# P.V gathered over three pairs of key tiles, and ten neighbourhood P buffers

## The chip, the cores and the metric

The kernel runs on one core of one Trainium2 chip. The metric is the time of one execution in microseconds of device time. Three runs of the kernel before took 2532.98, 2533.22 and 2537.31 us; the median is 2533.22 us. The engines are named as in the profile: PE (matrix multiplication), PEld (its weight loads), DVE, ACT, POOL and SP.

## The reference

One layer over 2048 latent tokens (a grid of 32 rows by 64 columns) with 256 context tokens. Two token mixers run on the same modulated input and are merged, projected and added to the stream:

```
oa = block_attention(qa, concat(ka, kca), concat(va, vca), mla_scale)   # 8 heads, DK 96, DV 64, all 2048+256 keys
ob = neighborhood_attention(qb, kb, vb, c_kb, c_vb, rpb)                # 8 heads of 64, window 8x16 + 256 context keys
y  = (sigmoid(ga) * ((oa * silu(za)) @ w_oa) + sigmoid(gb) * ((ob * silu(zb)) @ w_ob)) @ w_out
out = rmsnorm(x + gate * y, final_g)
```

Both mixers are a softmax over scores followed by a product P.V with the values, all in float32 accuracy.

## The kernel before, in words

The program has three stages one after the other: the input projections (up to about 1055 us of the span), the two attentions (about 1055 to 2157 us), and the output projections. The change touches the attention stage alone.

**The large attention.** It is a loop over 32 units: 8 heads by 4 blocks of 512 queries. A unit goes through 18 tiles of 128 keys in 9 steps of a pair (`for kp in range(NKP)`). A step computes two score tiles `S` on PE (three matmuls each, the operands being split into a high and a low part), each read by ACT, which writes `exp` into the step's tile `P` (one of `PB = 8` buffers). POOL adds `P` to the running sum `za` (line 1288). In the same steps PE computes `pm`, the scores of the next unit, 20 tiles of 512 or 256 columns spread over steps 0 to 5, and DVE takes their maxima `m` (line 825). From these DVE folds, POOL spreads (`md`, line 812) and PE makes the row `pmf` in step 8, which the next unit's scores need.

**P.V.** `pv(u, kp, ...)` is called one step late, for the pair of the step before. It puts the pair into the list `late`, and when `kp % PVB == PVB - 1`, or at the last pair, it issues the matmuls of every listed pair into `acc`. A pair's two tiles go to partitions 0 to 63 and 64 to 127 of `acc`, each with a stationary operand 64 columns wide, so the two run beside each other in the two column halves of the array. Every other matmul of the steps has a stationary operand 128 columns wide, but for sums over `za` (`zp`, `nz`), which are 32 wide. A float32 matmul shows as two instructions in the trace, so a pair is four `oacc` instructions.

**The neighbourhood attention** is a generator, `natten`, whose work is fed into the same steps by weight (`feed`): per head 24 maxima tiles `nm` with 8 `nc`, four spreads `nmd` on POOL each followed by a matmul `nf`, then 24 score tiles `ns` in 12 pairs. A score tile becomes a tile `np` (tag `P` of the pool `npl`, `NPB` buffers of 2 KB a partition), which POOL adds to `nza`. Its P.V, `n_pv` (result `no`), is 64 wide too. A pair first waits in `queue` behind the next pair, then in `held`; after each burst of P.V the loop empties `held` behind it, and where more than `HELD = 2` pairs are held, the oldest is issued at once. At the end of a head what is left is issued, the result is copied out, and the next head's keys and queries are loaded.

**Order.** PE's instructions of the loop are kept in program order (`pe["pin"]`). The other engines' orders are a planner's. Score tiles of every kind rotate through five PSUM buffers (`psm`: three of `psM`, two of `psS`), so PE waits when the tile five places back has not yet been read. `acc` has one buffer.

With `PVB = 2` a unit's P.V is issued behind the scores of steps 2, 4, 6, 8 and of step 0 of the next unit, with 2, 2, 2, 2 and 1 pairs.

Of the kernel before, what the change touches and what calls it, by code (L numbers as in the profile page):

```python
# [48 lines left out]
LEAD = 3  # L49
TAIL = 6  # L50
FILL = 16
PVB = 2
X0P = True
NATP = (2, 4)
STAT0 = 300
# [1 line left out]
HELD = 2  # L57
PB = 8
ZDVE = {1: tuple(range(1, 9))}
NPB = 6  # L60
BIG = -float(2 ** 100)


# [1 line left out]
def tile_hybrid_layer(ctx: ExitStack, tc: tile.TileContext, I: dict, out: bass.AP, dbg=None):  # L65
# [74 lines left out]
    def psm(name):  # L140
        if env["rot"] is not None:
            env["rot"] = (env["rot"] + 1) % 5
            if env["rot"] >= 3:
                return env["psS"].tile([P, W], F32, tag="S", name=name)
        return psM.tile([P, W], F32, tag="M", name=name)
# [778 lines left out]
    def n_score(d, t):  # L924
        h = d["h"]
        ps = psm(f"ns{h}_{t}")
        pt = npl.tile([P, W], F32, tag="P", name=f"np{h}_{t}", bufs=NPB)
        za = d["za"]
# [300 lines left out]
    def pv(u, kp, pt, acc, za, vt):  # L1229
        late.append((kp, pt))  # L1230
        if kp % PVB == PVB - 1 or kp == NKP - 1:
            env["burst"] = True
# [311 lines left out]
```

## Time and profile before

| | us |
|---|---|
| median of three runs | 2533.22 |
| profiled execution | 2537.19 |
| its span, first to last instruction | 2535.4 |
| PE busy in the span | 2489.2 (98%) |
| POOL / DVE / ACT busy in the span | 1093.5 / 1105.9 / 903.1 |
| mean granted TensorE clock | 0.995 |

The profile is of one execution on the chip. Busy times of PE come from modelled ends: matmuls are pipelined, so a matmul of 512 columns shows 0.40 us, while the next one starts 0.23 to 0.24 us after it. What PE spends is therefore read from the starts. Idle time of an engine costs something only where another engine waits for it.

### The profile page before, as it was taken

What the parts mean: (1) busy time and instruction counts of PE and PEld (TensorE: products, weight loads), DVE (VectorE), ACT (ScalarE), POOL (GpSimd) and SP (SyncE); (2) the same over time, 40 slices, a digit from 0 to 9 for tenths busy, and PEclk for the clock granted to TensorE, in tenths of its full rate; (3) what the DMA queues carried; (4) which work ended last, traced back from release to release, by engine and by line L of the source; (5) the groups of instructions that cost most, each with busy time, mean ns of one, the idle gap of its engine ahead of it and who ended that gap; (6) DMA issues with size and microseconds to landing.
All of it is one profiled execution on the core that took longest, in us unless ns stands there. A gap on an engine that the chain in (4) does not pass through costs nothing.

```text
span 2535.4 us, 34849 instructions
## 1 busy us (share of the span) xinstructions
PE 2489.2 (98%) x12796; PEld 1833.4 (72%) x12796; DVE 1105.9 (44%) x2285; ACT 903.1 (36%) x1774; POOL 1093.5 (43%) x861
## 2 busy tenths in 40 slices
PE   7999999999999999999999999999999999999998
PEld 4878888877789888756566656565656564888998
DVE  4654221222311211255465545465545446455654
ACT  4664432212322122234444444444444444112221
POOL 1312111111310000268877878777878886133220
PEclk9999999999999999999999999999999999999999
DMA  7535766456652466631415141514150333755542
GB/s 269 191 94 166 253 225 193 126 164 192 191 167 89 121 208 209 177 85 47 100 33 129 39 110 39 121 38 110 39 129 15 76 135 123 262 184 164 179 146 71
DMA packets 182979, 342.86 MB, mean 135 GB/s; under 512 B 25130, under 2 KB 95950, under 8 KB 175438
## 3 DMA queue, kind: packets, MB, share of 16 engines
q1 hardware_dynamic: 168872, 299.01, 39.5%
q0 software_dynamic: 13504, 41.35, 5.8%
q8 instruction: 100, 1.64, 0.3%
q14 instruction: 71, 0.58, 0.1%
q10 hardware_dynamic: 432, 0.28, 0.0%
HBM read 214.42 MB, written 126.13 MB: 134 GB/s over the span
## 4 chain that ended last, share of the span: by engine, by line
PE 89%; DMA 3%; DVE 3%; SPq 1%; ACT 1%; issue 1%; POOL 1%; POOLq 0%; DVEq 0%; ACTq 0%
PE accm L135 26%; PE S L807 15%; PE oacc L807 10%; PE pm L807 6%; PE f L135 5%; PE ya L135 4%; PE vacc L135 4%; PE nacc L226 3%; PE no L807 3%; PE accf L135 2%; PE accx L135 1%; PE nm L807 1%; DMA rz<-rzS 1%; PE pstl L185 1%; PE qa_False L135 1%
## 5 line engine op out<-in xcount | busy, mean ns | idle before, releaser
L1288 POOL TENSOR_TENSOR za<-za,P 128x1024 f32<-128x1024 f32 x217 | 516.3, 2379 | 111.2 <-ACT P L1278 107.5
L825 DVE TENSOR_REDUCE m<-pm 128x1 f32<-128x512 f32 (+1 forms) x640 | 388.1, 632 | 327.2 <-PE pm L807 320.6
L1278 ACT ACTIVATE P<-S 128x512 f32<-128x512 f32 x576 | 342.1, 596 | 452.4 <-PE S L807 432.7
L135 PE MATMUL accm<-hh,whi 128*128 128x512 f32 x928 | 366.8, 395 | 0.0
L135 PE MATMUL accm<-hl,whi 128*128 128x512 f32 x928 | 366.5, 395 | 0.0
L135 PE MATMUL accm<-hh,wlo 128*128 128x512 f32 x928 | 366.5, 395 | 0.0
L807 PE MATMUL oacc<-P,V 128*64 128x512 f32 x1152 | 286.7, 614 | 0.0
L807 PE MATMUL S<-qh,Kh 97*128 97x512 f32 x576 | 238.5, 414 | 3.9 <-DVE m L825 1.5
L807 PE MATMUL S<-ql,Kh 96*128 96x512 f32 x576 | 229.5, 398 | 0.0
L807 PE MATMUL pm<-Kh,qh 96*128 96x512 f32 (+1 forms) x640 | 223.5, 388 | 4.9 <-ACT P L1278 2.7
L807 PE MATMUL S<-qh,Kl 96*128 96x512 f32 x576 | 228.3, 396 | 0.0
L135 PEld LDWEIGHTS accm<-hh,whi 128*128 128x128 f32 x928 | 174.2, 188 | 42.8 <-issue 0.8
L135 PEld LDWEIGHTS accm<-hh,wlo 128*128 128x128 f32 x928 | 174.2, 188 | 42.4
L135 PEld LDWEIGHTS accm<-hl,whi 128*128 128x128 f32 x928 | 174.2, 188 | 41.4
L135 PE MATMUL ya<-u,woh 128*128 128x256 f32 x1024 | 185.0, 283 | 1.7 <-DVE t L1346 1.7
L807 PEld LDWEIGHTS pm<-Kh,qh 96*128 96x128 f32 x640 | 120.2, 188 | 90.5 <-issue 37.5
L807 PEld LDWEIGHTS oacc<-P,V 128*64 128x64 f32 x1152 | 69.5, 137 | 134.4 <-issue 133.6
L135 PE MATMUL f<-wfh,y 128*128 128x512 f32 (+1 forms) x528 | 161.6, 386 | 5.0 <-ACT y L1349 2.9
L135 PEld LDWEIGHTS ya<-u,woh 128*128 128x128 f32 x1024 | 160.1, 192 | 2.9 <-DVE t L1346 2.1
L135 PE MATMUL ya<-u,wol 128*128 128x256 f32 x512 | 144.9, 283 | 0.0
L807 PEld LDWEIGHTS S<-qh,Kh 97*128 97x128 f32 x576 | 109.4, 190 | 48.3 <-issue 16.9
L356 ACT ACTIVATE g<-accm 128x512 f32<-128x512 f32 x88 | 52.1, 592 | 249.5 <-PE accm L135 201.9
(1928 smaller groups left out, 4248.9 us busy)
## 6 DMA issues: line engine op xcount, KB each, us to landing
rawc<-in_wch SPq DMA_DIRECT2D x30, 512.0 KB
KA<-kB SPq DMA_DIRECT2D x16, 576.0 KB
xl<-in_xb SPq DMA_DIRECT2D x32, 256.0 KB
wm<-in_wmodb SPq DMA_DIRECT2D x8, 1024.0 KB
kmS<-sk POOLq DMA_DIRECT2D x32, 256.0 KB, 3.7
qR<-q SPq DMA_DIRECT2D x16, 512.0 KB
qm<-sq POOLq DMA_DIRECT2D x32, 256.0 KB, 3.9
woS<-ps SPq DMA_DIRECT2D x16, 512.0 KB
```

The source lines that it names most:

```text
L135: nc.tensor.matmul(acc, a, b, start=(i == 0), stop=(i == n - 1))
L185: nc.tensor.matmul(pst[32 * j:32 * j + 32, :w], ones[:, 0:32], sq[:, :w], start=(kt < 4), stop=(kt >= 4))
L226: nc.tensor.matmul(acc[:, :n], a[:, k, sl], b[:, k, :n], start=(k == 0 and q == 0), stop=(k == KT - 1 and q == 2))
L356: nc.scalar.activation(s1, acc, AF.Sigmoid)
L807: ins = nc.tensor.matmul(*args, **kw)
L825: nc.vector.reduce_max(m5[:, qt, ci:ci + 1], pm[:, :b - a], axis=AX.X)
L1278: nc.scalar.activation(pt[:, x, :], sp, AF.Exp)
L1288: ve.tensor_tensor(za, za, pt, op=ALU.add)
```

## The change

Two constants change. P.V is issued after three pairs, with 3, 3 and 3 pairs a unit, behind the scores of steps 3 and 6 and of step 0 of the next unit. The neighbourhood's `P` has ten buffers, 8 KB a partition more.

```diff
-PVB = 2
+PVB = 3
...
-NPB = 6
+NPB = 10
```

## Rows read from the trace of the kernel before

**Rows 1.** The page: span, PE's busy line, the chain that ended last.
```profile
span 2535.4 us, 34849 instructions
PE 2489.2 (98%) x12796; PEld 1833.4 (72%) x12796; DVE 1105.9 (44%) x2285; ACT 903.1 (36%) x1774; POOL 1093.5 (43%) x861
...
PE 89%; DMA 3%; DVE 3%; SPq 1%; ACT 1%; issue 1%; POOL 1%; POOLq 0%; DVEq 0%; ACTq 0%
```

**Rows 2.** Engines by stretch, the part of the loop with neighbourhood work.
```profile
core 0: us, PE busy (x) PEld busy (x) DVE busy (x) ACT busy (x) POOL busy (x), PEclk, DMA share, GB/s
...
1090.00:2100.00 1010.00, 998.75 (x4927) 614.60 (x4925) 543.06 (x1099) 451.81 (x816) 807.22 (x482) 0.99 0.31 78
```

**Rows 3.** Waits of PE, 1055 to 2157 us: total, times, longest us.
```profile
PE nf L807 <- POOL nmd L812: 3.9, 3, 2.7
PE pmf L807 <- POOL md L812: 3.2, 1, 3.2
PE pm L807 <- ACT P L1278: 2.7, 4, 0.7
PE pm L807 <- DVE m L825: 1.8, 3, 0.8
```

**Rows 4.** Timeline of PE (start, us, instruction, count): two pairs between wide matmuls.
```profile
1525.18 0.39 PE L807 MATMUL S<-ql,Kh 96*128 96x512 f32 x1
1525.42 0.39 PE L807 MATMUL S<-qh,Kl 96*128 96x512 f32 x1
1525.64 0.39 PE L807 MATMUL pm<-Kh,qh 96*128 96x512 f32 x1
1525.96 1.94 PE L807 MATMUL oacc<-P,V 128*64 128x512 f32 x8
1527.83 0.50 PE L807 MATMUL pm<-Kh,qh 96*128 96x512 f32 x1
1528.17 0.30 PE L807 MATMUL ns_('w', 0, 0)_12607<-QQ,KA 128*128 128x288 f32 x1
```

**Rows 5.** Timeline: one pair alone; two pairs with a neighbourhood pair.
```profile
1517.74 1.94 PE L807 MATMUL oacc<-P,V 128*64 128x512 f32 x8
1519.51 0.59 PE L807 MATMUL no<-np_('c', 0, 1)_12355,nv 128*64 128x512 f32 x1
...
1520.46 0.39 PE L807 MATMUL pm<-Kh,qh 96*128 96x256 f32 x1
...
1614.15 1.08 PE L807 MATMUL oacc<-P,V 128*64 128x512 f32 x4
1615.16 0.50 PE L807 MATMUL pm<-Kh,qh 96*128 96x512 f32 x1
```

**Rows 6.** Engines in three stretches of one unit between two bursts.
```profile
1511.91:1517.74 5.83, 5.83 (x28) 4.56 (x26) 5.17 (x11) 3.12 (x6) 2.35 (x1) 1.00 0.11 25
1520.46:1525.96 5.50, 5.50 (x27) 4.35 (x26) 4.58 (x10) 2.51 (x5) 3.13 (x2) 1.00 0.00 0
1527.83:1533.20 5.37, 5.37 (x29) 4.08 (x29) 4.14 (x10) 2.75 (x6) 4.66 (x3) 1.00 0.01 3
```

**Rows 7.** Timeline of PE at the first nf; idle before it in brackets.
```profile
1103.67 0.79 PE L807 MATMUL nf<-nmd,onesr 128*128 128x512 f32 x1 [2.67 <-POOL nmd L812]
```

**Rows 8.** PE busy, granted clock and DMA by stretch, after that and at 1618.
```profile
1103.70:1106.70 3.00, 3.00 (x7) 0.50 0.86 172
1106.70:1109.70 3.00, 3.00 (x9) 0.54 0.00 0
...
1618.00:1624.00 6.00, 4.68 (x16) 0.79 0.57 155
```

**Rows 9.** Waits in the loop: the longest for neighbourhood P.V.
```profile
DVE np_('w', 1, 3)_16453 L953 <- PE no L807: 4.4, 1, 4.4
```

**Rows 10.** Engines by stretch, while a head's operands are loaded.
```profile
1839.00:1863.00 24.00, 24.00 (x134) 13.69 (x133) 8.88 (x17) 11.03 (x19) 19.62 (x12) 1.00 1.01 231
```

**Rows 11.** The page's group of DVE's maxima: busy, mean ns, idle before.
```profile
L825 DVE TENSOR_REDUCE m<-pm 128x1 f32<-128x512 f32 (+1 forms) x640 | 388.1, 632 | 327.2 <-PE pm L807 320.6
```

## The prediction

> **What bounds the kernel now.** I read the page first: the profiled execution has a span of 2535.4 us (its own time is 2537.19, so 1.8 lie around the span), PE is busy for 98% of it and holds 89% of the chain that ended last [rows 1]. The reader is to see there that time can only be won on PE. The engines by stretch come next, for the attention loop: POOL is busy 807.2 of 1010 us, DVE 543.1, ACT 451.8, at a granted clock of 0.99 [rows 2]. They have slack, POOL the least with 20%. The waits of PE say how much of the loop is not PE's own work: the four largest sums are 3.9, 3.2, 2.7 and 1.8 us in 1102 us [rows 3]. So the loop, 1102 of the 2535 us, is a queue of matmuls in a fixed order, and its length is the sum of the distances from one start to the next. The timeline of PE gives these, and it is where the change is decided.
>
> **Part 1, PVB: what a separate burst costs.** Wide matmuls of 512 columns follow each other at (1525.64 - 1525.18) / 2 = 0.23 us. The first P.V matmul starts 0.32 after the last wide one: 0.09 lost on the way in. The first wide one after the burst is followed by the next at 0.34 instead of 0.23: 0.11 lost behind it [rows 4]. The burst itself, from its first start to the next wide start: one pair takes 1615.16 - 1614.15 = 1.01, two take 1527.83 - 1525.96 = 1.87, two with a neighbourhood context pair (as much work as a third) take 1520.46 - 1517.74 = 2.72 [rows 4, 5]. That is 0.855 a pair and a remainder of 0.155 that does not grow with the length. A burst costs 0.09 + 0.155 + 0.11 = 0.355 us whatever it holds; I take 0.35. Four starts read to 0.01 us put it between 0.33 and 0.37. No other engine can hide it: PE has no idle time there, it is the array that changes between 64 and 128 wide.
>
> The Trainium skill says of this change of width that "Changing tiling mode (not just tile) drains the TensorE" (TensorEngine Tiling (Array Packing), Key Properties). TensorE: Matmul & The Clock Gate (Single matmul latency, Back-to-back issue gap) gives an isolated matmul (398 + N) / 2.4 ns and one in a stream N / 2.4 + 2.5, so that a drain would be some 163 ns and a burst with two of them 0.33 us, an estimate; the sum would be 61 x 0.33 = 19.9 us. The trace has 0.355, and I go by it.
>
> **How many bursts go.** Walked through the loops as written: before, 32 units x 5 = 160 bursts, the last two with nothing between them, so 159; 7 of the 8 flushes of neighbourhood P.V at a head's end stand alone: 166. After: 32 x 3 = 96; the 8 head ends then all stand alone, and once a third pair is held (HELD = 2) and goes out by itself: 105. So 61 go, and 61 x 0.35 = 21.4 us (20.1 to 22.6). The matmuls themselves are the same in number and kind, so nothing else changes in PE's own work. The bursts of 32-wide sums (zp, nz) stay.
>
> **The longer stretch between bursts.** During a burst DVE and ACT catch up; between bursts PE produces score tiles that they must read within five tiles. In three two-step stretches DVE worked 5.17 of 5.83, 4.58 of 5.50 and 4.14 of 5.37 us [rows 6]: always below PE, so a third step adds no backlog on average. What is new is steps 1 to 3 in one stretch. They hold 10 maxima against 7 in steps 1 and 2; the third step's 3 cost DVE 3 x 0.632 = 1.9 us [rows 11], and with a neighbourhood share (DVE's 543.1 us [rows 2] over 288 x 1010 / 1102 = 264 steps are 2.05 a step, less 2.2 maxima, 0.65) 2.55, about what PE needs for half a two-step stretch (2.7). The second group, steps 4 to 6, ends with a step without maxima. Bounds: a loss of as much again as PE waits for ACT and DVE in the rows, 2.7 + 1.8 = 4.5 [rows 3], or a gain of 4.5 where the present waits fall into longer bursts. I take a loss of 1.5, since DVE's share is nearer to full than to half.
>
> **The matmuls nf and pmf, which wait for POOL.** POOL spreads the maxima, and PE then waits at nf (3.9 us in all) or pmf (3.2) [rows 3]. For pmf the distance holds: the burst of step 6 lies between in both kernels, and it has three pairs instead of two. For nf, walked again, 7 of 32 have a burst between spread and matmul now, 4 after. Three lose their cover. Below, nothing; above, three waits as long as the longest, 2.67 [rows 7]. Behind that wait the granted clock was 0.50 and 0.54, that is 1.2 GHz for nearly all of 6 us [rows 8], which loses some 2.9. So 3 x 5.6 = 16.8 above. I take 1, because 3 waits in 32 are listed now though 25 have no cover. Queued behind a waiting nf is all of PE, and through it everyone.
>
> **Part 2, ten buffers.** With bursts further apart up to eight neighbourhood tiles are alive at once (counted in the same walk), so six would not do. The longest wait of DVE for such a buffer was 4.4 us [rows 9]; with ten these waits go. DVE is not PE's bound there, so the gain is between 0 and the 1.8 for which PE waits for DVE [rows 3]; I take 0, as none of those waits names such a tile. The 8 KB lie in a pool that is closed before the output projections, and no instruction or transfer is added.
>
> **The loads at a head's end.** They are issued behind the head's last scores, as before. In one head they kept the DMA engines at 1.01 for the 24 us up to the next head's first scores [rows 10]. The transfers do not get faster while PE comes earlier: 24 us are about 6.3 steps of 3.8 us, which hold 3.5 bursts now and 2.1 after, 1.4 x 0.35 = 0.5 us. Seven heads at most: 0 to 3.5 us; I take 0.5, one head as tight as this one. SP's and POOL's queues get nothing new, and no queue is passed. The end of the loop is unchanged: the last two bursts already are one.
>
> **The sum**, against the profiled execution: 2537.2 - 21.4 + 1.5 + 1 + 0 + 0.5 = 2518.8. That execution is 4.0 above the median of 2533.2, so the forecast is 2514.8, about 2515 us, or 0.7% faster.
>
> **Rivals.**
> 1. *The reads become the bound.* In steps 1 to 3 DVE falls behind, and PE stops at the fifth tile. For it: DVE at 89% in the first row [rows 6], and waits of about 0.6 us for it (1.8 in three) [rows 3]. Against: the other two stretches, 83 and 77%. Price: one such wait in half of the 64 stretches that hold maxima, 32 x 0.6 = 19 us; with the other terms 2534, no change.
> 2. *Idle PE loses its clock: slower.* Three idle places in the loop already did: [rows 8] show two of them. If the spreads on POOL (80% busy now, 82% at the shorter loop) come later than PE at nf and pmf, each event costs 2.67 + 2.9 = 5.6 us. The forecast's 18.4 are gone from the fourth new event (22.4), and with five the kernel is at 2515 + 28 = 2543. Place: the 63 nf and pmf matmuls. Against: pmf keeps its cover.
>    The Trainium skill has the same in TensorE: Matmul & The Clock Gate (HAM oscillation): an idle array falls back to half rate, and only activity releases it. The 0.50 of the rows agrees.
> 3. *The bursts do not merge.* If more than two pairs were held nearly always, neighbourhood P.V would go out by itself, and every such pair would cost the 0.35 that was won; 61 of the 96 pairs would do it, and the time would be 2533. Against: the walk finds one.
> 4. *Better than forecast.* Of the present waits most vanish, with a lucky order on DVE: another 8 us, 2507 or below.
>
> **How the numbers follow.** Forecast 0.80, rivals 1 to 4: 0.06, 0.05, 0.04, 0.05. The forecast's own range: downwards the burst's price (1.2) and the waits (1.5 + 4.5) to 2508; upwards the waits (3), one new clock event (5.6) and late loads (2) to 2526. That holds 8 in 10 by itself: 2508 to 2526. A measurement of this kernel tells about 0.2%, 5 us, from no change, so faster means below 2528: the forecast, rival 4 and a little of rival 1, 0.86. Within 0.2%: most of rivals 1 and 3 with a fifth of rival 2, 0.10. Slower: the rest of rival 2, 0.04.
>
> **What would show it.** P.V in runs of 12 instructions; no run of 4 or 8 inside the loop; the distances 0.32, 0.34 and 0.855 a pair unchanged, so that a run of three pairs lasts 2.72. The loop, from first score to last P.V, 18 to 21 us shorter than 1102, and the other two stages the same to 1 us. If the loop's shortening is smaller, PE's waits for DVE m or ACT P must have grown by it (rival 1), or POOL nmd and md with more time at clock 0.50 (rival 2). The forecast is wrong if the 0.35 does not go with the burst, that is if a run of three pairs takes longer than 2.72.

## The result and the profile after

The changed kernel takes 2520.27 us, median of its runs (2518.12 to 2524.23), against 2534.36 for the kernel before (2532.98 to 2537.31). The ratio is 0.9943, 95% interval 0.9929 to 0.9956: 14.1 us faster, 0.56%. The forecast was 2515, 18.4 faster. The direction, the size to within 5 us and the price and number of the bursts were right; two terms of the sum were not, and part of the nearness is luck, as the last parts show.

The profiled execution took 2524.23, 13.0 less than the one of before. First the page of the changed kernel: span, busy times, the chain's shares and the group of DVE's maxima.

```profile
span 2522.5 us, 34848 instructions
PE 2476.6 (98%) x12796; PEld 1841.1 (73%) x12796; DVE 1108.0 (44%) x2285; ACT 900.8 (36%) x1774; POOL 1092.7 (43%) x861
...
PE 91%; DVE 3%; DMA 2%; ACT 2%; issue 1%; POOL 1%; SPq 0%; POOLq 0%; ACTq 0%; DVEq 0%
...
L825 DVE TENSOR_REDUCE m<-pm 128x1 f32<-128x512 f32 (+1 forms) x640 | 385.9, 632 | 284.4 <-PE pm L807 278.0
```

Beside [rows 1, 11]: the same 12,796 matmuls and 12.6 us less of PE's busy time. DVE, ACT and POOL differ by at most 2.3 us, the weight loads show 7.7 more. A maximum still takes 632 ns.

Next the timeline of PE in the changed kernel around one burst (start, us, instruction, count), beside [rows 4]:

```profile
1120.70 0.40 PE L807 MATMUL S<-qh,Kl 96*128 96x512 f32 x1
1120.93 0.40 PE L807 MATMUL pm<-Kh,qh 96*128 96x512 f32 x1
1121.26 2.79 PE L807 MATMUL oacc<-P,V 128*64 128x512 f32 x12
1123.98 0.50 PE L807 MATMUL pm<-Kh,qh 96*128 96x512 f32 x1
1124.32 0.39 PE L807 MATMUL ns_('c', 2, 1)_9052<-QQ,KA 128*128 128x512 f32 x1
```

Three pairs are one run of 12. It begins 0.33 after the last wide matmul, lasts 1123.98 - 1121.26 = 2.72, and the second wide one behind it starts 0.34 after the first: the entry, the length and the exit that the prediction named. Counted over the loop there are 166 runs before and 105 after, as walked. The price of a run beyond its pairs, worked out from the starts of all runs that stand between wide matmuls, has a median of 0.349 us before and 0.350 after, for one, two and three pairs alike.

The waits of PE in the changed kernel, 1055 to 2157 us (total, times, longest), beside [rows 3]:

```profile
PE pm L807 <- DVE m L825: 5.8, 3, 3.5
PE S L807 <- ACT P L1278: 5.1, 6, 2.4
PE pm L807 <- ACT P L1278: 2.7, 4, 0.7
PE nf L807 <- POOL nmd L812: 2.1, 2, 1.9
PE S L807 <- DVE nmx L886: 1.1, 1, 1.1
```

POOL's waits shrank (nf 3.9 to 2.1, pmf 3.2 to none on the list). Those of `pm` for DVE's `m` grew from 1.8 to 5.8, and those of `S` for ACT's `P` from 0.4 to 5.1. Summed over all tiles, PE's waits went from 7.1 to 2.1 for POOL, from 4.8 to 8.4 for DVE and from 4.0 to 8.2 for ACT. The readers of PSUM have taken POOL's place.

**Where the 13 us lie.** By first score and last P.V, the profiled span splits into: before the loop 1055.6 to 1053.0 (-2.5), the loop 1100.8 to 1093.6 (-7.3), the output stage 379.0 to 375.9 (-3.1). The first is no effect of the change: before had a half-clock stretch of 3.4 us in its first stage, and among all executions of this study, whose first stages are the same code, it lasted 1050.9 to 1057.8. The loop holds -21.3 of bursts (61 x 0.35) and +14.0 of something else. Most of that are intervals between wide matmuls that are longer than the 0.23 of a stream. What they have too much, worked out from all starts, sums to 32.9 us before and 45.2 after:
- short ones at full clock, 60 to 200 ns too long: 81 (8.7 us) before, 122 (12.9 us) after, +4.2;
- long ones at full clock, over 200 ns: +4.6 in units 30 and 31 (5.7 to 10.3), +0.8 in all the others (16.3 to 17.1);
- intervals inside half-clock stretches: 1.9 to 4.0, +2.1; what is under 60 ns, +0.6.

The other 1.7 are bursts and narrower matmuls, in half-clock stretches mostly. Unit by unit the loop shows the same: units 0 to 27 are 15.6 us shorter, units 28 to 30 0.5, and unit 31, the last, is 8.9 us longer.

**The last two units.** The timeline of the changed kernel there, all engines, the lines that matter (idle before an instruction and what ended it in brackets):

```profile
2099.39 2.56 DVE L1106 TENSOR_TENSOR o<-o,z 128x256 f32<-128x256 f32 x1
...
2102.14 0.62 DVE L825 TENSOR_REDUCE m<-pm 128x1 f32<-128x512 f32 x1
...
2102.82 0.58 PE L807 MATMUL pm<-Kh,qh 96*128 96x256 f32 x1 [3.46 <-DVE m L825]
...
2123.28 0.42 DVE L1106 TENSOR_TENSOR o<-o,z 128x256 f32<-128x256 f32 x1 [0.32 <-DMA o<-oaS]
2123.74 0.42 ACT L1108 ACTIVATE u<-o 128x256 fp32r<-128x256 f32 x1 [1.34 <-DVE o L1106]
2124.18 2.07 ACT L1278 ACTIVATE P<-S 128x512 f32<-128x512 f32 x4
2124.82 0.50 PE L807 MATMUL S<-qh,Kh 97*128 97x512 f32 x1 [2.37 <-ACT P L1278]
...
2132.95 0.42 ACT L1108 ACTIVATE u<-o 128x256 fp32r<-128x256 f32 x1 [2.69 <-POOL o L1106]
2133.27 1.07 ACT L1278 ACTIVATE P<-S 128x512 f32<-128x512 f32 x2
2133.91 0.80 PE L807 MATMUL S<-qh,Kh 97*128 97x512 f32 x1 [1.83 <-ACT P L1278]
```

The reader is to see one pattern three times: a small instruction of the *next* stage stands in a reader's queue ahead of the work that PE waits for. `o`, `z` and `u` (lines 1105 to 1109, in `make_u`) prepare operands of the output projections, beside the last units. At 2102.82 (unit 30) PE had waited 3.46 for a maximum that stood behind DVE's `o`, and 1.60 at 2098.86 for another behind the `o` of 2095.90; before, the waits for DVE in that unit were 0.67, 0.63 and 0.43. In unit 31 there are no maxima any more, so the three-step stretch holds nothing but score tiles, each for ACT. ACT stood idle 1.34 and 2.69 us at a copy `u` whose `o` had not come, with the exps behind it, and PE ran out of its five buffers: 2.37 and 1.83 us. TensorE: Matmul & The Clock Gate, Part 1 (Architectural detail), in the Trainium skill, says that ACT's queue is strictly first in, first out; these rows agree, as the exps start 0.44 and 0.32 us after the copy, four and two in a row.

What followed on PE in the changed kernel, by stretch (PE's busy us first, then the other engines, granted clock, DMA):

```profile
core 0: us, PE busy (x) PEld busy (x) DVE busy (x) ACT busy (x) POOL busy (x), PEclk, DMA share, GB/s
2122.00:2125.00 3.00, 0.63 (x3) 0.19 (x3) 2.01 (x5) 1.64 (x4) 0.00 (x0) 1.00 0.50 158
2134.00:2140.50 6.50, 6.50 (x16) 2.97 (x18) 3.98 (x3) 2.67 (x6) 3.47 (x4) 0.50 0.36 111
```

In the first stretch PE is busy for 0.63 of 3 us. After the second idle place it worked for 6.5 us at a granted clock of 0.50, that is 1.2 GHz, with 16 matmul records in it. So 4.2 us of waits cost some 3.3 more (an estimate, half of the 6.5). In all, the loop spends 17.1 us at half clock before and 27.3 after. The wait of 3.2 for `pmf` in unit 30 of before [rows 3], with 6.8 us of half clock behind it, is gone; that is why unit 30 comes out even.

Part of it is given back behind the loop: the first final projection of before waits for a weight load, and after it does not. The row of before's output stage, then that of after:

```profile
PE f L135 <- DMA wfh<-wfS: 2.0, 1, 2.0
```

```profile
PE f L135 <- DMA wfl<-wfS: 0.5, 2, 0.3
```

What differs is when SP issues that load: at 2164.92 before, 8.5 us after the last P.V, and at 2151.00 after, 4.4 behind it. SP has the preparation of the next stage and the last store of `oaS` ahead of it in its queue, and in the changed kernel, whose last unit is 8.9 us longer, it is through with that earlier against the loop's end. Where the last unit is as short as before (e3, e4, e10), the issue is 9.0 to 10.6 us behind the last P.V and the wait is back.

### The profile page after: what moved, and what is told of

Its sections match the earlier page's. It is cut to its first block, busy times and chain, and to the rows that moved or that the text cites. A ratio compares the mean times of both kernels' runs of the same rounds, so it can differ in the third digit from the quotient of the medians.

```text
span 2522.5 us, 34848 instructions
## 1 busy us (share of the span) xinstructions
PE 2476.6 (98%) x12796; PEld 1841.1 (73%) x12796; DVE 1108.0 (44%) x2285; ACT 900.8 (36%) x1774; POOL 1092.7 (43%) x861
## 4 chain that ended last, share of the span: by engine, by line
PE 91%; DVE 3%; DMA 2%; ACT 2%; issue 1%; POOL 1%; SPq 0%; POOLq 0%; ACTq 0%; DVEq 0%
PE accm L135 26%; PE S L807 16%; PE oacc L807 10%; PE pm L807 5%; PE ya L135 5%; PE f L135 4%; PE vacc L135 4%; PE nacc L226 3%; PE no L807 3%; PE accf L135 2%; PE accx L135 1%; PE nm L807 1%; PE pstl L185 1%; PE qa_False L135 1%; ACT P L1278 1%
## 5 line engine op out<-in xcount | busy, mean ns | idle before, releaser
L807 PE MATMUL oacc<-P,V 128*64 128x512 f32 x1152 | 274.9, 613 | 0.0
L807 PE MATMUL pm<-Kh,qh 96*128 96x512 f32 (+1 forms) x640 | 214.5, 382 | 8.7 <-DVE m L825 5.8
L807 PEld LDWEIGHTS oacc<-P,V 128*64 128x64 f32 x1152 | 75.7, 139 | 150.1 <-issue 150.1
L807 PEld LDWEIGHTS S<-qh,Kh 97*128 97x128 f32 x576 | 109.5, 190 | 56.8 <-ACT P L1278 22.6
```

The lines of the kernel that those rows point to most:

```text
L807: ins = nc.tensor.matmul(*args, **kw)
```

## The experiments

"Loop" is first score to last P.V of the profiled execution (before 1100.8, changed 1093.6), "short" the number and sum of the short intervals at full clock (before 81 and 8.7, changed 122 and 12.9; the expectations counted those inside half-clock stretches too, 89 and 138). The time is a ratio to the kernel before on the same chip, with its interval.

| run | P.V bursts | ratio | loop, us | short (us) |
|---|---|---|---|---|
| e1_pvb1 | 294 | 1.0092 [1.0077, 1.0107] | 1129.6 | 21 (2.1) |
| e2_npb10 | 166 | 0.9985 [0.9976, 0.9994] | 1097.9 | 82 (8.7) |
| e3_last2 | 108 | 0.9924 [0.9911, 0.9936] | 1082.4 | 116 (12.5) |
| e4_ucopy | 105 | 0.9917 [0.9904, 0.9931] | 1081.8 | 122 (13.0) |
| e5_before_ucopy | 166 | 0.9990 [0.998, 1.0] | 1097.7 | 81 (8.7) |
| e6_pvb5 | 75 | 0.9921 [0.9908, 0.9934] | 1083.6 | 136 (14.5) |
| e7_merge678 | 136 | 0.9961 [0.9946, 0.9976] | 1091.3 | 88 (9.5) |
| e8_after | 105 | 0.9935 [0.9921, 0.9949] | 1094.9 | 120 (12.8) |
| e9_moredve | 105 | 1.0142 [1.0119, 1.0164] | 1133.8 | 277 (30.6) |
| e10_last2_ucopy | 108 | 0.9933 [0.992, 0.9946] | 1082.3 | 116 (12.4) |
| e11_pvb5_last2_ucopy | 80 | 0.9914 [0.9898, 0.9929] | 1082.0 | 135 (14.6) |

**e1: every pair alone** (on the kernel before).
```diff
-PVB = 2
+PVB = 1
```


> The kernel before with PVB = 1: every pair is its own burst. Walked through the loops, 294 separate bursts of 64-wide matmuls in place of 166, 128 more. Theory A (a burst costs 0.35 us whatever it holds): 128 x 0.35 = 45 us more than before, about 2579, with one pair still lasting 1.01 us from its first start to the next wide matmul. Rival B (the price is hidden or shared where bursts are short, or the gain of the change came from something else than the number of bursts): clearly less than 45, say under 25 us.

2561.89 against 2538.19, +23.7. The price held: its timeline shows a burst of one pair in the same form,

```profile
1506.65 0.40 PE L807 MATMUL S<-qh,Kl 96*128 96x512 f32 x1
1506.98 1.08 PE L807 MATMUL oacc<-P,V 128*64 128x512 f32 x4
1507.99 0.50 PE L807 MATMUL S<-qh,Kh 97*128 97x512 f32 x1
1508.33 0.40 PE L807 MATMUL S<-ql,Kh 96*128 96x512 f32 x1
```

0.33 in, 1.01 long, 0.34 out, and over 193 such bursts the median is 0.348: 128 x 0.348 = 44.6 us added. But what the longer intervals of wide matmuls have too much fell from 32.9 to 17.1, so 15.8 of it did not show, and the loop is 28.8 longer (1129.6 to 1100.8). The time is up by less, and meets the mark of rival B (under 25). The trace says in which sense: the price itself is not hidden in PE, but waits go as bursts come. That is what the prediction's sum also lacked: bursts give the readers time, and taking them away brings waits.

**e2: the ten buffers alone** (on the kernel before).
```diff
-NPB = 6
+NPB = 10
```


> The kernel before with ten neighbourhood buffers alone (PVB stays 2). Theory A: PE's order is the same and the waits for such buffers are not PE's, so no change, within 2 us of before. Rival C (the buffers carry part of the gain, or of the loss): more than 4 us either way.

0.9985, some 3.8 us (1.5 to 6.1). The waits of [rows 9] are gone: five of DVE and ACT for PE to free a buffer, 14.6 us in all. PE's order is the same instruction for instruction, its short waits stay (82), and the units differ from before by more than 0.1 us in six places: units 1 (-1.1), 12 (+1.6), 16 (-1.6), 27 (-1.0), 30 (-3.0) and 31 (+2.1). In units 1, 12, 16 and 30 a half-clock stretch falls elsewhere; in unit 31 two new waits of 0.71 and 0.84 stand before P.V. In unit 30 PE's clock fell at 2110.4, ahead of `pmf`, which then came in time, instead of after a wait for it; e5 has -2.6 there with six buffers.

Unit 27 is the place of the buffers. The timeline of the kernel before:

```profile
2006.67 0.50 PE L807 MATMUL pm<-Kh,qh 96*128 96x512 f32 x1 [0.69 <-ACT P L1278]
...
2009.98 0.60 ACT L935 ACTIVATE np_('c', 1, 1)_16845<-ns_('c', 1, 1)_16844 128x512 f32<-128x512 f32 x1 [3.37 <-PE no L807]
```

The `ns` tile was ready at 2004.1, but its reader on ACT stood without a buffer until the neighbourhood's P.V, so one of the five PSUM tiles stayed unread for 6 us, and PE stopped for 0.69 at a `pm`. With ten buffers that read runs as soon as the tile is ready, and PE's wait is gone; e5, with six, keeps it. So the trace has about 1 us for the buffers, and the rest of the timed 3.8 has no place in it.

**e3: the last two units at two pairs** (on the changed kernel).
```diff
-        if kp % PVB == PVB - 1 or kp == NKP - 1:
+        pvb = 2 if u >= nu - 2 else PVB
+        if kp % pvb == pvb - 1 or kp == NKP - 1:
```


> The changed kernel, but units 30 and 31 gather two pairs again. 3 bursts more than the changed kernel, about 1 us. Theory T (what is missing of the 21 us is lost at the end of the loop, where PE with three-step stretches overruns ACT and DVE, idles and drops to half clock): the last unit gets its 9 us back against the profile of the changed kernel, and the time falls to about 2514 to 2517, 4 to 6 us under the changed kernel's 2520.3. Rival D (the missing part is lost evenly in the stretches of all units): 1 us slower than the changed kernel, 2521.

Unit 31 falls from +8.9 to +1.7 against before, and no wait of `S` for ACT is left there. The loop is 11.2 us shorter than the changed kernel's 1093.6, of which 7.2 are unit 31 and 3.5 lie in units 0 to 27, whose work is the same and which spend 6.8 us less at half clock; the output stage takes 381.3 instead of 375.9, with the wait for `wfh` back.

**e4: the `u` copies off ACT** (on the changed kernel).
```diff
-                nc.scalar.activation(u[:, 0, :], o_, AF.Copy)
+                if tb < 2:
+                    nc.vector.tensor_copy(u[:, 0, :], o_)
+                else:
+                    nc.scalar.activation(u[:, 0, :], o_, AF.Copy)
```


> The changed kernel, but the copies u of the output projections' first two blocks (line 1108) run on DVE instead of ACT, so ACT's exp does not stand behind copies that wait for DVE, POOL or a DMA. Theory T1 (the place of these copies in ACT's queue makes the idle time in unit 31): PE's waits for ACT P in the last unit (2.4 and 1.8 us in the changed kernel) and the half-clock stretch behind them go, 5 to 8 us faster than the changed kernel, about 2514. Rival T2 (with three-step stretches and no maxima tiles in unit 31 PE runs out of PSUM buffers in any case): the waits stay, time within 2 us of 2520.

This takes away what stood ahead of the exps and leaves the three-pair order alone. Unit 31 is at +1.0, and PE has no wait at all in it; PE's busy time, clock and DMA in 30 us of the last unit:

```profile
core 0: us, PE busy (x), PEclk, DMA share, GB/s
2108.00:2138.00 30.00, 30.00 (x139) 1.00 0.37 108
```

That the `u` copies in ACT's queue were the cause of the last unit's loss is thereby shown, from two sides (e3, e4). The loop is 11.8 us shorter, 7.9 of it in unit 31; the output stage takes 379.0. By time neither e3 (expected 4 to 6 us under the changed kernel) nor e4 (5 to 8) is told apart from it: 0.9924 and 0.9917 against 0.9935 for e8, with overlapping intervals.

**e5: the same on the kernel before**, as a control (the edit of e4).

> The kernel before with the copies u of the first two output blocks on DVE. Theory T1 (these copies only hurt with three-step stretches, where no P.V covers ACT's wait in unit 31): within 2 us of before. Rival (they hurt always): 4 us or more faster than before, and then the gain of that edit on the changed kernel is not the change's own loss.

0.9990, at most 5 us, and the loop 3.1 shorter, most of it unit 30. With two pairs a burst the copies hardly matter.

**e6: five pairs** (on the changed kernel).
```diff
-PVB = 3
+PVB = 5
...
-HELD = 2
+HELD = 3
```


> The changed kernel with PVB = 5 and HELD = 3: P.V in bursts of 5 and 4 pairs, walked 75 bursts instead of 105, 30 fewer, 10.5 us less for the bursts. Theory W (each further step of a stretch with maxima tiles makes PE wait again for the readers of its PSUM tiles, ACT and DVE): the short waits rise to 180 or more and the longer ones too, so that 6 to 15 us are given back and the time is 2515 to 2525, about the changed kernel's. Rival E (the waits were the loop's end alone): 10 us faster than the changed kernel.

30 bursts fewer than the changed kernel, 10.5 us by the price; short waits rise to 136 (14.5 us), those of step 6 now lying in step 4 (4.1), fewer in number than the 180 expected. The time is 0.9921, whose interval overlaps that of the changed kernel. In units 0 to 27 the profile is 7.1 us shorter than that of the changed kernel (956.2 to 963.4) for 27 bursts, 0.26 each. So the trace still shows a gain below the full price, and the times can't tell it.

**e7: bursts behind the pairs of steps 1, 3, 5 and 8** (on the changed kernel). Steps 7 and 8, which have no maxima, join the start of step 0, which has two `pm` tiles ahead of its burst.
```diff
-PVB = 3
+PVB = (1, 3, 5, 8)
...
-        if kp % PVB == PVB - 1 or kp == NKP - 1:
+        if kp in PVB:
```


> Bursts behind pairs 1, 3, 5 and 8: as in the kernel before, but the burst of step 8 (pairs 6, 7) goes into that of step 0 (pairs 6, 7, 8), where there are no maxima tiles between them. Ten buffers. Walked 136 bursts, 30 fewer than before: 10.5 us. Theory W (waits come from stretches with maxima tiles): short waits stay near 89 and the full 9 to 11 us arrive, about 2524 to 2527. Rival F (any third step adds waits): 3 us or more of it are lost and short waits appear in steps 7, 8 and 0.

30 bursts fewer than before, 10.5 us by the price, and 0.9961 is 9.9 us (6.1 to 13.7). This kernel has ten buffers, which alone measured 3.8 (1.5 to 6.1) in e2, so the time by itself does not show that all is kept. The trace does: in units 0 to 27, which the end of the loop does not touch, e7 is 9.7 us shorter than e2 (967.4 to 977.1) for 27 bursts, 0.36 each, while the changed kernel is 13.7 shorter (963.4) for 54, 0.25 each. Short waits are 88, near before's 81; those in step 0 rise from 0.1 to 1.3 us, as rival F would have it there. A burst is worth its full price where the readers have slack, and here that is where hardly any maxima are.

The waits of PE's weight loads for ACT's exps, 1055 to 2157 us, which precede the matmul that is late, agree in part. The row of `S` before, changed and e7:

```profile
PEld S L807 <- ACT P L1278: 9.0, 25, 0.8
```

```profile
PEld S L807 <- ACT P L1278: 22.6, 51, 2.8
```

```profile
PEld S L807 <- ACT P L1278: 9.6, 24, 0.8
```

Of the 22.6, 5.1 are the two long waits of unit 31. The row of `pm` for the same exps goes the other way, 12.5, 4.4 and 3.3, so that both together are 21.5, 27.0 and 12.9: e7 has the least, but the rise from before to changed is smaller than the first row shows.

**e8: the changed kernel again.**

> The changed kernel again, unchanged, so that it shares the runs of before with the next three. All theories: 12 to 17 us under before, and in the profile about 138 short waits of PE (60 to 200 ns) inside the wide stretches against 89 before.

Another execution has unit 31 at +8.94, and units 2 to 30 differ by under 0.05 us each from the first; only unit 1 differs, by 1.3. The waits belong to the order of the work and are no accident.

**e9: more work for DVE** (on the changed kernel): each maxima tile gets a second reduction of 128 columns, whose output nothing reads.
```diff
+        jk1 = mq.tile([P, 1], F32, tag="jk1", ...)
...
             nc.vector.reduce_max(..., pm, ...)
+            nc.vector.reduce_max(jk1, pm[:, 0:P], axis=AX.X)
```


> The changed kernel with one more reduction on DVE per maxima tile (128 of its columns, into a tile that nobody reads), some 0.2 us each, 640 of them: DVE gets about 20% more work in the loop. Theory W (PE's short waits come from a backlog on DVE, and on ACT behind it, in stretches with maxima tiles): the short waits rise well above 144, the longer ones too, and the time by 8 us or more, to 2528 or above. Rival (ACT alone sets them, its exp being the reader): short waits stay near 140 and the time within 3 us of the changed kernel.

DVE's busy time in 990 us of the loop rises from 537 in the changed kernel to 618 (changed, then e9; busy time first):

```profile
1090.00:2080.00 990.00, 536.51 (x1089) 0.99 0.31 79
```

```profile
1090.00:2080.00 990.00, 617.67 (x1610) 1.00 0.29 68
```

and PE pays for it in the loop (its waits in e9, weight loads first):

```profile
PEld S L807 <- DVE jk L827: 20.9, 45, 2.0
...
PEld S L807 <- ACT P L1280: 17.6, 44, 1.1
...
PEld pm L807 <- DVE jk L827: 11.8, 30, 1.8
...
PE S L807 <- DVE jk L827: 5.3, 12, 1.7
```

The loop is 40 us longer though DVE is busy for only 62% of it, and the short waits go from 122 to 277. So DVE is a second bound, in single steps, while its average says that there is slack of a third. The second reduction also holds its `pm` tile longer itself; how much of the loss is that and how much a backlog behind it, e9 does not separate.

**e10: e3 and e4 together.**

> The changed kernel with both edits to the loop's end: two pairs a burst in units 30 and 31, and the copies u of the first two output blocks on DVE. If each already takes the 9 us out of unit 31, they don't add: loop 18 to 20 us shorter than before, and 3 to 5 us of it lost again at the first final matmul, which then waits for the load of wfh: 18 to 20 us under before. If they add, 24 or more.

Loop 1082.3, like each alone; the output stage is 381.3, and its first projection waits longer for its weights:

```profile
PE f L135 <- DMA wfh<-wfS: 3.6, 1, 3.6
```

The edits don't add, since both remove the same wait.

**e11: five pairs, the last two units at two, the copies on DVE.**

The diff is that of e3, e4 and e6 together.

> PVB = 5, HELD = 3, two pairs a burst in units 30 and 31, copies u on DVE. Theory W with the loop's end mended: 5 and 4 pairs save some 26 bursts more than 3 (9 us) and lose about half of it to more waits in stretches with maxima tiles: 3 to 5 us under e10, 22 to 25 under before. If the waits eat all of it: as e10.

2515.01, 0.9914: the lowest of the study, and 21.8 us below the kernel before. Its interval (0.9898 to 0.9929) overlaps that of the changed kernel (0.9921 to 0.9949), so it is the best candidate and not a shown improvement on it. Its profiled loop (1082.0) is no shorter than that of e10: units 0 to 27 are 8.6 us shorter, but units 28 to 31 are 8.3 longer, with a wait of 4.0 in unit 31, where P.V stands until DVE has read `acc` (`or`).

## Why the prediction was nearly right, by its steps

**Right.** *The price of a burst* (0.35) and *that it does not grow with the length*: 0.348 to 0.350 in three kernels with one, two and three pairs. The estimate worked out from the Trainium skill's TensorE: Matmul & The Clock Gate was 0.33, and the trace's 0.35 decides. That a drain of the array makes the price is not shown by any run. *How many go*: 61. *A run of three lasts 2.72*: it does. *Rival 3*, that bursts would not merge, is out.

**The longer stretch: mis-sized.** It stood at +1.5 and measured +4.2 in short waits (+4.1 in e8), beside the last units' +4.6 in long ones. The prediction compared DVE's work with PE's time over whole two-step stretches [rows 6] and found 77 to 89%, "always below PE", so "a third step adds no backlog on average". That is true of the average and was the wrong question: PE is only five tiles ahead, so what counts is each step. By step, the short waits were 2.1, 0.2, 3.5, 0.9 and 0.6 us in steps 2 to 6 before, and are 2.9, 1.8, 0.6, 3.2 and 1.9: a burst behind step 3 relieves step 4, but the steps that have become the second and third of a stretch (2 and 3, 5 and 6) lose more. Step 0, now the third behind 7 and 8, went from 0.1 to 1.4. e7, which joins steps 7, 8 and 0 alone, nearly keeps the old sum (9.5 to 8.7). Which reader is late in these steps is argued and not shown: e9 shows that PE feels a longer read on DVE, but by name PE's weight loads wait for ACT's exps most. Of the 122, 72 lie on the second matmul of a score tile, which waits for nothing itself: 46 of them follow a first matmul that was late. A late one costs some 0.10 us more at the next, as a burst does at its exit, and the waits by name do not show this. Rival 1, the readers as the bound, was put at 0.06 and at 19 us; it came in at 9 (4.2 + 4.6), half of it in the last two units.

**"The end of the loop is unchanged": failed.** This step looked at P.V bursts alone, and the last burst of each unit does stay as it was. But units 30 and 31 have another load on DVE and ACT, the operands of the next stage, and a longer stretch without a break meets it: +8.9 us in unit 31, cause shown by e3 and e4. Half clock makes up a part of it (6.8 us in unit 31, none there in e4), as rival 2 said in kind, though not at the place that it named: `nf` and `pmf` wait less than before.

**The `nf` cover (+1), the buffers (0), the head loads (+0.5).** `nf` waits fell from 3.9 to 2.1, so the +1 was on the wrong side by 2.8. The buffers measured -3.8 by e2 (1.5 to 6.1), of which the trace places about 1 us. The prediction looked for them in PE's waits for DVE; the buffer that cost PE time was ACT's (3.4 in unit 27), and PE's wait stood under the name of an exp. No new wait at a head's loads shows.

**The sum, then**, for the profiled loop: -21.3, +4.2 short waits, +5.4 long ones, +4.4 half clock and small change, is -7.3, where the prediction had -18.4. The output stage's -3.1 and the first stage's -2.5 make up 5.6, where it had none ("the other two stages the same to 1 us"): a late weight load stood at the head of the output stage. The profiled time was forecast at 2518.8 and came to 2524.2, 11.1 - 5.6 = 5.5 more. So the near miss is partly luck: two errors oppose each other, and the first stage's 2.5 are no effect of the change.

**What stays open.** Repairing the last unit takes 7.2 to 9.5 us out of it (the profiled loops are 11 to 12 shorter, the rest in units with the same work), of which 3 to 5 go back into the output stage; the timed kernels gain 0.5 to 4.6 over the changed one (e3, e4, e10 against e8, by the ratios), and the intervals overlap. The profiled loops differ by a few us with where half-clock stretches fall, and timed runs need not have them in the same place. Most of the timed gain of the buffers is open too.

## To carry over

Price a burst by its entry and exit in the timeline, and count bursts: that part comes out to 2%. Then ask for each step that a longer stretch joins whether its *readers* are ahead in that step, since busy shares of a stretch hide a queue that is only five tiles deep: in units 0 to 27 the 112 bursts between one and two pairs were worth 23.4 / 112 = 0.21 us each instead of 0.35, and where steps 7, 8 and 0 were joined (e7 against e2), 9.7 / 27 = 0.36. And look at the units that lack the usual filler, first and last, with the next stage's preparation in the same queues: what stands there ahead of a PSUM reader sets PE's time.

## Not expected of the hardware

A small product of 128x256 on DVE took 0.35 to 0.43 us alone, and 2.57 beside an addition of POOL, with whose end it nearly ended. The timeline of the changed kernel:

```profile
2113.04 4.88 POOL L1288 TENSOR_TENSOR za<-za,P 128x1024 f32<-128x1024 f32 x2 [2.78 <-ACT P L1278]
...
2115.62 2.57 DVE L1105 TENSOR_TENSOR z<-z,rz 128x256 f32<-128x256 f32 x1
```

2115.62 + 2.57 = 2118.19, and POOL's two additions end at 2117.92; DVE's 2.56 us of `o` at 2099.39, behind which the maximum stood that PE waited for, ran beside POOL in the same way. Of the 32 products `z` and `o` on DVE in the loop, before and changed together, 13 started while a POOL instruction ran, and each of them ended 0.27 to 0.29 after that instruction; the other 19 took 0.35 to 0.43. The Trainium skill (SBUF — State Buffer, Terms) says that the two share a pair of ports that one of them holds for a whole instruction while the other is blocked. So POOL, off the critical path, set a wait of PE through DVE.
